# Tokens scaled ahead of their transposes, the first two products interleaved, and the residual's scale taken out later

## Chip, cores and metric

One core of one Trainium2 chip runs the kernel. The metric is the device time of one execution in microseconds (us). Before the change the median of three runs is 1152.77 us (1152.27 to 1153.73).

## What is computed

One inference step of a two-layer decoder for 512 prompt tokens and 8 x 8 sample tokens, 576 columns in all, with 1024 features. Layer A is a gated linear recurrence of 16 heads of 128 keys and 128 values; then come one shared key/value projection, layer B (sliding-window attention over it) and a last norm. What the change touches is the entry into layer A:

```python
def rms_norm(x, g):
    y = x * lax.rsqrt(jnp.mean(x * x, axis=-1, keepdims=True) + EPS)
    return y * g
def hgrn2_layer(x, s0, w_in, w_out, g_norm, g_onorm, lb):
    q, fz, i, gate = jnp.split(rms_norm(x, g_norm) @ w_in, 4, axis=-1)
    logf = jnp.logaddexp(jnp.log(lb), jnp.log1p(-lb) + jax.nn.log_sigmoid(fz))
    k = (1.0 - lb) * jax.nn.sigmoid(-fz)
    q = jax.nn.silu(q) * A_HEAD_K ** -0.5
    o, s_new = hgrn2_recurrence(heads(q), heads(k), heads(i), heads(logf), s0)
    o = rms_norm(o, g_onorm) * jax.nn.silu(gate)
    return x + o @ w_out, s_new
```

The last line needs the residual x itself, not the normed x.

## The kernel before

Activations lie with features on partitions: hT, xhi and xlo are 128 x 8 x 576 (8 feature tiles k, 576 columns in two halves j of 288). A product with a 1024 x 128 slice of weights is made of three terms of rounded numbers: whi·xhi, whi·xlo and wlo·xhi, 8 tiles by 2 halves each, 48 matmuls of 128 x 288. The weights come by SP's DMA queue into a tile raw (three buffers); ACT rounds it to whi (line 205) and DVE takes wlo = raw - whi (line 209). In layer B, wlo is made by another way: ACT writes -whi, and a DMA that POOL issues adds raw to it (lines 202 and 203).

The beginning (lines 154 to 306): SP loads three token blocks xt of 128 x 1024, six small vectors into vecs, two more token blocks, then weights. `arrive(i)` sums a block's squares on ACT, transposes the raw block on PE in eight pieces (px, line 281), copies them to hT on DVE (line 282), turns the sum into the reciprocal root q on ACT (lines 283 and 284), and spreads q along the columns of rall: a diagonal dg on DVE (line 286), multiplied with ones on PE (pr, line 288), copied by ACT (line 289). `normed(j)` then makes, for each k of a half, u = hT·norm_a·rall on DVE (line 296), xhi on ACT (line 297) and xlo = u - xhi on DVE, or on POOL for k in 1, 4, 7 (line 298):

```python
        for k in range(KT):
            u = stp.tile([P, HN], F32, tag="u", name=f"u{j}_{k}", bufs=4)
            dve.scalar_tensor_tensor(u, hT[:, k, r], vec("norm_a", k), rall[:, r], ALU.mult, ALU.mult)
            act.copy(xhi[:, k, r], u)
            (pool if k in LO_POOL else dve).tensor_tensor(xlo[:, k, r], u, xhi[:, k, r].bitcast(F32), ALU.subtract)
```

`head_main(h)` makes a head's four products, pf (forget), pq (query), pi (value) and pg (gate), each with its elementwise work: from pf come ka, lf, the sums Xl (five adds on POOL, line 611) and a scan NB; from pq comes KQ. Head 0's pf is made half by half, all other products with both halves in turn. `head_rec(h)` is the recurrence of a head: the factors G and KL, E, kd, Qz and KQ·E on DVE and ACT, then small matmuls (pa, poT, psO, pus). It is woven with head_main(h + 1), so that PE makes the next head's products between the small matmuls. The output of a head is normed per token: ACT squares psO and poT into `on` with a sum (line 900), takes Ln and Exp (lines 901 and 902), and scales psO and poT into `on` (line 904), which also ends their use of PSUM; the pool of PSUM tiles named psx has three buffers, which px, poT, psO, pus and others share. The second pus takes the buffer that psO held. A scheduler in the framework orders each engine's instructions by readiness and by priorities that the code gives; `tc.issue_after(x)` puts work behind the instruction x on the same engine. Every engine runs its list in order. After every fourth head the residual is brought up to date (hT += po, line 443).

## Time and profile before

| | |
|---|---|
| median of 3 runs | 1152.77 us |
| profiled execution: its own time | 1152.44 us |
| profiled execution: span of the profile | 1150.6 us |
| mean granted TensorE clock | 0.987 |
| PE, DVE, ACT, POOL busy | 1105.9, 857.6, 749.4, 265.9 us |

The span is the part of the profiled execution that the trace covers; its own time is 1.84 us longer. PE is the matmul engine, DVE, ACT and POOL do elementwise work, SP issues most DMAs. Rows of a timeline say when an instruction (or xN of a kind in a row) starts, how long it takes, the engine, the line of the code, what it writes and reads, and in brackets how long the engine had been idle before it and what ended that. "PEclk" is the granted share of the full TensorE clock.

### The profile page before, as it was taken

The numbers are of one execution on the slowest core, as the hardware profiler recorded it, in microseconds if no ns is written. First come the engines' busy times: TensorE is split into PE (matmuls) and PEld (weight loads), VectorE is DVE, ScalarE is ACT, GpSimd is POOL, SyncE is SP. The second block draws the span as 40 slices with busy tenths as digits, with TensorE's granted clock in tenths as the row PEclk, the third lists the DMA queues.
The fourth block names the chain that finished last, engine by engine and source line by source line (L and its number), as shares of the span: only waits on it lengthen the run. The fifth ranks groups of instructions, "written<-read, shape, count | busy, mean of one in ns | idle before, by whom it ended". The sixth has DMA issues, their size and how long they took to land.

```text
span 1150.6 us, 27472 instructions
## 1 busy us (share of the span) xinstructions
PE 1105.9 (96%) x10937; PEld 1072.6 (93%) x10937; DVE 857.6 (75%) x2090; ACT 749.4 (65%) x1748; POOL 265.9 (23%) x311
## 2 busy tenths in 40 slices
...
GB/s 157 93 113 78 104 94 113 77 79 108 71 118 107 122 87 110 89 76 107 96 71 110 86 77 92 143 137 117 132 114 126 129 128 134 126 127 113 127 111 83
DMA packets 168010, 123.19 MB, mean 107 GB/s; under 512 B 4665, under 2 KB 158314, under 8 KB 167850
## 3 DMA queue, kind: packets, MB, share of 16 engines
...
q14 instruction: 42, 0.34, 0.1%
...
## 4 chain that ended last, share of the span: by engine, by line
PE 51%; DVE 6%; ACT 3%; issue 1%; DMA 1%; POOL 0%; DVEq 0%; POOLq 0%; ACTq 0%
PE pbg L216 8%; PE pbq L216 8%; PE po L216 6%; PE po L233 4%; PE pg L233 3%; PE pf L233 3%; PE pi L233 3%; PE pq L233 2%; PE sc L1103 2%; PE pkv L216 2%; PE pav L1186 1%; PE pz L216 1%; PE pa L802 1%; PE ptr L1154 1%; DMA wlo_o<-raw_o 1%
## 5 line engine op out<-in xcount | busy, mean ns | idle before, releaser
L205 ACT CAST whi_a<-raw_a 128x1024 fp32r<-128x1024 f32 x64 | 67.1, 1049 | 66.8 <-PE po L233 32.3
L209 DVE TENSOR_TENSOR wlo_a<-raw_a,whi_a 128x1024 fp32r<-128x1024 f32 x64 | 81.8, 1284 | 24.6 <-issue 23.2
L611 POOL TENSOR_TENSOR Xl<-Xl 128x72 f32<-128x72 f32 x80 | 49.6, 649 | 207.0 <-DVE Xl L608 205.7
L643 POOL TENSOR_TENSOR sg<-sg,lg 128x576 f32<-128x576 f32 x16 | 26.2, 1638 | 279.3 <-ACT lg L576 279.3
L1132 ACT ACTIVATE P<-P,st 128x192 f32<-128x192 f32 (+2 forms) x128 | 54.1, 424 | 38.4 <-DVE st L1127 38.3
L1141 POOL TENSOR_SCALAR P<-P,st 128x192 f32<-128x192 f32 (+1 forms) x64 | 47.9, 754 | 93.6 <-DVE st L1134 76.8
L443 DVE TENSOR_TENSOR hT<-hT,po 128x576 f32<-128x576 f32 x32 | 24.1, 754 | 51.0 <-PE po L233 50.7
L233 PE MATMUL po<-oh,whi_o 128*128 128x288 f32 x256 | 42.8, 302 | 4.4 <-ACT whi_o L205 1.9
L216 PE MATMUL po<-ohb,wlo_o 128*128 128x288 f32 x224 | 41.1, 297 | 2.2 <-DMA wlo_o<-raw_o 2.1
L667 POOL TENSOR_TENSOR vb<-vst,bmask 128x512 fp32r<-128x512 f32 x32 | 36.7, 1166 | 26.7 <-DVE vst L663 13.8
L216 PE MATMUL po<-ohb,whi_o 128*128 128x288 f32 x224 | 42.0, 302 | 0.2
L216 PE MATMUL pbq<-xhi,wlo_bq 128*128 128x256 f32 (+1 forms) x256 | 39.9, 297 | 2.4 <-DMA wlo_bq<-raw_bq 2.4
L233 PEld LDWEIGHTS po<-oh,whi_o 128*128 128x128 f32 x256 | 35.9, 188 | 6.4 <-ACT whi_o L205 2.2
L216 PE MATMUL po<-olb,whi_o 128*128 128x288 f32 x224 | 41.4, 298 | 0.5 <-DVE olb L1400 0.4
L233 PE MATMUL po<-ol,whi_o 128*128 128x288 f32 x256 | 41.4, 299 | 0.0
L233 PE MATMUL po<-oh,wlo_o 128*128 128x288 f32 x256 | 41.1, 298 | 0.0
L216 PE MATMUL pbq<-xhi,whi_bq 128*128 128x256 f32 (+1 forms) x256 | 40.5, 300 | 0.0
L216 PE MATMUL pbg<-xhi,whi_bg 128*128 128x288 f32 x256 | 40.5, 300 | 0.0
L216 PE MATMUL pbq<-xlo,whi_bq 128*128 128x256 f32 (+1 forms) x256 | 39.3, 296 | 0.0
L233 PE MATMUL pf<-xhi,wlo_a 128*128 128x288 f32 x256 | 37.5, 299 | 1.8 <-DVE wlo_a L209 1.8
L216 PE MATMUL pbg<-xhi,wlo_bg 128*128 128x288 f32 x256 | 39.1, 295 | 0.0
L233 PE MATMUL pf<-xhi,whi_a 128*128 128x288 f32 x256 | 39.1, 303 | 0.0
(390 smaller groups left out, 3676.7 us busy)
## 6 DMA issues: line engine op xcount, KB each, us to landing
...
```

Source lines behind the costliest of these rows:

```text
L205: act.copy(hi[:, :n], raw[:, :n])
L209: eng.tensor_tensor(lo[:, r], raw[:, r], hi[:, r].bitcast(F32), ALU.subtract)
L216: pe.matmul(pm[:, : c1 - c0], w[:, k * width + w0 : k * width + w0 + P], x(k)[i][:, c0:c1], start=n == 0, stop=n == len(terms) - 1,)
L233: pe.matmul(pm[:, j, :HN], w[:, k * width + c0 : k * width + c0 + P], x(k, j), start=n == 0 and k == 0, stop=n == 2 and k == nk - 1,)
L443: dve.tensor_add(h2, h2, ps2(pm))
L611: pool.tensor_tensor(X8[:, :, j : j + 1], X8[:, :, j : j + 1], X8[:, :, k : k + 1], ALU.add)
L643: (pool if SGP else dve).tensor_tensor(sg, sg, l, ALU.mult)
L667: pool.tensor_tensor(t, view(vst.bitcast(F32), [[0, 4], [1, P]], off=half * P), view(bmask, [[1, 4], [0, P]]), ALU.mult,)
L802: pe.matmul(pa[32 * j : 32 * j + ns, c, t0 : t0 + nt], keys[:, c * P + s0 : c * P + s0 + ns], queries[:, c * P + t0 : c * P + t0 + nt], st ...
L1103: pe.matmul(sc[:, hf, k0[hf] :], QS[pr][:, 2 * n + hf, :], kk[:, g, ks], start=q == 0, stop=q == 1)
L1132: act.activation(x, x, AF.Exp, bias=st[:, a : a + 1], accum_out=st[:, 8 + a : 9 + a])
L1141: (pool if e == "p" else dve).tensor_scalar(x, x, st[:, 8 + a : 9 + a], None, ALU.mult)
```

## The change

The vector norm_a is loaded by itself behind the first token block, and the first two weight slices ahead of the other vectors. Each token block is multiplied by its q in place, tokens on partitions, before it is transposed, so that hT holds normed tokens. xhi is then one ACT instruction from hT with norm_a as scale, and xlo one DVE instruction. wlo of head 0's first two slices is made by ACT and a POOL DMA, as in layer B. Head 0's pf and pq are interleaved by k in the first half. The small constants on DVE are put behind the last xlo. rall now holds 1/q; it is made after pq, and hT gets its scale back in 16 multiplications of 128 x 288, four in each of heads 0 to 3.

```diff
--- before.py
+++ after.py
@@ -67,7 +67,6 @@
-LO_POOL = (1, 4, 7)
@@ -157,29 +156,36 @@
         sp.dma_start(xt[:n, :], tokens(i))
         xts.append(xt)
 
-    for i in range(3):
+    load_tokens(0)
+    vec_a = stp.tile([KT, P], F32, name="vec_a")
+    sp.dma_start(vec_a, norm_a.rearrange("o (k p) -> (o k) p", p=P))
+    for i in range(1, 5):
         load_tokens(i)
 
+    raws = {}
+    for part in (1, 0):
+        src = w_in_a[0, :, part * DI : part * DI + P].rearrange("(k p) c -> p k c", p=P)
+        raws[f"a0_{part}"] = wts.tile([P, 1024], F32, tag="raw", name=f"raw_a0_{part}", bufs=3)
+        sp.dma_start(raws[f"a0_{part}"].rearrange("p (a c) -> p a c", a=KT), src)
+
+
     vecs = stp.tile([64, P], F32, name="vecs")
-    dve.memset(vecs, 0.0)
-    row = 0
-    vcol = {}
+    pool.memset(vecs, 0.0)
+    row = KT
+    vcol = {"norm_a": (0, KT)}
     for name, ap, n in (
-        ("norm_a", norm_a.rearrange("o (k p) -> (o k) p", p=P), KT),
         ("norm_kv", norm_kv.rearrange("(k p) -> k p", p=P), KT),
         ("norm_b", norm_b.rearrange("o (k p) -> (o k) p", p=P), KT),
         ("norm_f", norm_f.rearrange("(k p) -> k p", p=P), KT),
         ("lb", lower_bounds_a.rearrange("o (k p) -> (o k) p", p=P), NH),
         ("onorm", onorm_a, 1),
     ):
-        sp.dma_start(vecs[row : row + n, :], ap)
+        sp.dma_start(vecs[row - KT : row - KT + n, :], ap)
         vcol[name] = (row, n)
         row += n
-    for i in range(3, 5):
-        load_tokens(i)
     snk = cst.tile([P, NHB], F32, name="snk")
     sp.dma_start(snk, bass.AP(tensor=sinks_b.tensor, offset=sinks_b.offset, ap=[[0, P], [1, NHB]]))
-    vT = cst.tile([P, 64], F32, name="vT")
+    vT = cst.tile([P, KT + 64], F32, name="vT")
 
     def vec(name, i):
         r, _ = vcol[name]
@@ -268,91 +274,120 @@
     rts = [rall[:, j * HN : (j + 1) * HN] for j in range(2)]
     ssq = cst.tile([P, 5], F32, name="ssq")
 
+    def to_tokens(i, after):
+
+        n = P if i < 4 else LS
+        q = ssq[:n, i : i + 1]
+        junk = stp.tile([P, D], F32, tag="junk", name=f"junk{i}", bufs=2)
+        act.activation(junk[:n], xts[i][:n], AF.Square, accum_out=q)
+        act.activation(q, q, AF.Ln, bias=eps_c[:n], scale=1.0 / D)
+        act.activation(q, q, AF.Exp, scale=-0.5)
+        with ExitStack() as when:
+            if after:
+                when.enter_context(tc.issue_after(after))
+            dve.tensor_scalar(xts[i][:n], xts[i][:n], q, None, ALU.mult)
+
     def arrive(i):
 
         n = P if i < 4 else LS
-        xt, q = xts[i][:n], ssq[:n, i : i + 1]
         r = slice(i * P, i * P + n)
-        junk = stp.tile([P, D], F32, tag="junk", name=f"junk{i}", bufs=2)
-        act.activation(junk[:n], xt, AF.Square, accum_out=q)
         for c in range(0, KT, 4):
             px = misc(f"px{i}_{c}").rearrange("p (k t) -> p k t", k=4)[:, :, :n]
             for k in range(4):
-                pe.transpose(px[:, k, :], xt[:, (c + k) * P : (c + k + 1) * P], ident[:n, :n])
-            dve.tensor_copy(hT[:, c : c + 4, r], px)
-        act.activation(q, q, AF.Ln, bias=eps_c[:n], scale=1.0 / D)
-        act.activation(q, q, AF.Exp, scale=-0.5)
-        dg = stp.tile([P, P], F32, tag="dg", name=f"dg{i}", bufs=2)
-        dve.tensor_scalar(dg[:n, :n], ident[:n, :n], q, None, ALU.mult)
-        pr = half(f"pr{i}")
-        pe.matmul(pr[:, :n], ones[:n, :], dg[:n, :n], start=True, stop=True)
-        act.copy(rall[:, r], pr[:, :n])
-
-    def normed(j):
+                pe.transpose(px[:, k, :], xts[i][:n, (c + k) * P : (c + k + 1) * P], ident[:n, :n])
+            last = dve.tensor_copy(hT[:, c : c + 4, r], px)
+        return last.ins
+
+    def normed(j, ks):
 
         r = slice(j * HN, (j + 1) * HN)
-        for k in range(KT):
-            u = stp.tile([P, HN], F32, tag="u", name=f"u{j}_{k}", bufs=4)
-            dve.scalar_tensor_tensor(u, hT[:, k, r], vec("norm_a", k), rall[:, r], ALU.mult, ALU.mult)
-            act.copy(xhi[:, k, r], u)
-            (pool if k in LO_POOL else dve).tensor_tensor(xlo[:, k, r], u, xhi[:, k, r].bitcast(F32), ALU.subtract)
-
-    for i in range(3):
+        for k in ks:
+            high = act.activation(xhi[:, k, r], hT[:, k, r], AF.Copy, scale=vec("norm_a", k))
+            low = dve.scalar_tensor_tensor(
+                xlo[:, k, r], hT[:, k, r], vec("norm_a", k), xhi[:, k, r].bitcast(F32), ALU.mult, ALU.subtract
+            )
+        return high.ins, low.ins
+
+    def high(name):
+
+        hi, lo = [wts.tile([P, 1024], F32R, tag=t, name=f"{t}_{name}") for t in ("whi", "wlo")]
+        act.copy(hi, raws[name])
+        return hi, lo
+
+    def low(name, hi, lo):
+        act.activation(lo, raws[name], AF.Copy, scale=-1.0)
+        pool.dma_start(lo.bitcast(F32), raws[name], accum_op=ALU.add)
+
+    pv = misc("pva")
+    pe.transpose(pv[:, :KT], vec_a, ident[:KT, :KT])
+    dve.tensor_copy(vT[:, :KT], pv[:, :KT])
+    came = []
+    for i in range(5):
+        to_tokens(i, came[i - 2] if i > 1 else None)
+        if i < 3:
+            came.append(arrive(i))
+    w0 = {1: high("a0_1")}
+    normed(0, range(3))
+    w0[0] = high("a0_0")
+    first, _ = normed(0, range(3, KT))
+    with tc.issue_after(first):
+        low("a0_1", *w0[1])
+    for i in range(3, 5):
         arrive(i)
+    low("a0_0", *w0[0])
+    _, second = normed(1, range(KT))
     pv = misc("pv")
     pe.transpose(pv[:, :64], vecs, ident[:64, :64])
-    dve.tensor_copy(vT, pv[:, :64])
-    normed(0)
-    for i in range(3, 5):
-        arrive(i)
-    normed(1)
-
...
     si = cst.tile([P, P], I32, name="si")
     ti = cst.tile([P, P], I32, name="ti")
     pool.iota(si, [[0, P]], base=0, channel_multiplier=1)
     pool.iota(ti, [[1, P]], base=0, channel_multiplier=0)
-
...
+    with tc.issue_after(second):
...
     amask = cst.tile([P, W], F32, name="amask")
@@ -580,14 +615,59 @@
             c = part * DI + h * P
             return split_weights(w_in_a[0, :, c : c + P].rearrange("(k p) c -> p k c", p=P), f"a{h}_{part}")
 
+        def again():
+
+            for i in range(5):
+                n = P if i < 4 else LS
+                if i in (0, 4):
+                    pr = misc(f"pr{i}")
+                c = i % 4 * P
+                pe.matmul(pr[:, c : c + n], ones[:n, :], dg[:n, i * P : i * P + n], start=True, stop=True)
+                if i > 2:
+                    act.copy(rall[:, i // 4 * LP : (i + 1) * P if i < 4 else T], pr[:, : c + n])
+
+        dg = tt("dg")
+        with tc.issue_after(second):
+            dve.reciprocal(ssq[:, :4], ssq[:, :4])
+            dve.reciprocal(ssq[:LS, 4:], ssq[:LS, 4:])
+            for i in range(5):
+                n = P if i < 4 else LS
+                dve.tensor_scalar(dg[:n, i * P : i * P + n], ident[:n, :n], ssq[:n, i : i + 1], None, ALU.mult)
+
+        def first_two():
+
+            pms = {p: main(f"p{'qf'[p]}0") for p in (1, 0)}
+
+            def terms(p, j, ws):
+                for k, w, x in ws:
+                    pe.matmul(
+                        pms[p][:, j, :HN],
+                        w0[p][w][:, k * P : (k + 1) * P],
+                        xview((xhi, xlo)[x])(k, j),
+                        start=k == 0 and w == 0 and x == 0,
+                        stop=k == KT - 1 and (w, x) == ((1, 0), (0, 1))[j],
+                    )
+
+            for k in range(KT):
+                for p in (1, 0):
+                    terms(p, 0, [(k, 0, 0), (k, 0, 1)])
+            for p in (1, 0):
+                terms(p, 0, [(k, 1, 0) for k in range(KT)])
+                terms(p, 1, [(k, w, x) for k in range(KT) for w, x in ((0, 0), (1, 0), (0, 1))])
+            return pms[1], pms[0]
+
         def head_main(h, st):
             KQ = wk.tile([P, 2, T], F32, tag="KQ", name=f"KQ{h}", bufs=2)
             NB = wk.tile([P, 2, T], F32, tag="NB", name=f"NB{h}", bufs=2)
             st["KQ"], st["NB"] = KQ, NB
 
-            w = weights_in(h, 1)
-            pf = main(f"pf{h}")
-            yield from product(pf, *w, xview(xhi), xview(xlo), order=((0, 1),) if h else ((0,), (1,)))
+            if h:
+                w = weights_in(h, 1)
+                pf = main(f"pf{h}")
+                yield from product(pf, *w, xview(xhi), xview(xlo))
+            else:
+                pf, pq = first_two()
+                again()
             with early():
                 l = tt(f"lf{h}")
                 act.activation(s2(l), ps2(pf), AF.Abs)
@@ -612,9 +692,10 @@
             dve.tensor_tensor_scan(NB[:, 1, :], rmask, lf, 0.0, ALU.mult, ALU.add)
             yield
 
-            w = weights_in(h, 0)
-            pq = main(f"pq{h}")
-            yield from product(pq, *w, xview(xhi), xview(xlo))
+            if h:
+                w = weights_in(h, 0)
+                pq = main(f"pq{h}")
+                yield from product(pq, *w, xview(xhi), xview(xlo))
             with early():
                 q = KQ[:, 1, :]
                 l = silu_arg(pq, q, f"q{h}")
@@ -818,7 +899,7 @@
                     stop=True,
                     tile_position=(0, 32 * j),
                 )
-            dve.copy_predicated(att, view(m_ge, [[0, NC], [1, P]]), pa)
+            st["mark"] = dve.copy_predicated(att, view(m_ge, [[0, NC], [1, P]]), pa).ins
             ats = att_s[i2]
             dve.copy_predicated(
                 view(ats[:LS, :], [[32, 4], [1, 16]]),
@@ -974,6 +1055,11 @@
             woven(head_rec(h, st, outs), itertools.chain(*chunks), n)
             for make in {5: (prompt_mask,), 6: (sample_mask,), 7: (sink_rows,)}.get(h, ()):
                 make()
+            if h < 4:
+                with tc.issue_after(st["mark"]):
+                    for j in range(4):
+                        x = hT[:, 2 * h + j // 2, j % 2 * HN : j % 2 * HN + HN]
+                        dve.tensor_tensor(x, x, rts[j % 2], ALU.mult)
             st = nxt
         out_scaled(w_out_a, NH - 4 + FILL, outs[FILL:], "norm_kv", tt)
         share[0] = LO_KV
```

The order of the instructions, at three places.

PE at the beginning (px: transposed token blocks; pr: q spread over columns; xt_88 is block 0, xt_92 and xt_94 are blocks 1 and 2, xt_96 and xt_98 blocks 3 and 4). Before, from the third block on:

```order
L281 MATMUL px_0_158<-ident,xt_92 128x128 x4
L281 MATMUL px_4_164<-ident,xt_92 128x128 x4
L288 MATMUL pr_174<-dg_172,ones 128x128
L303 MATMUL pv<-ident,vecs 128x64
L281 MATMUL px_0_214<-ident,xt_102 128x128 x4
L281 MATMUL px_4_220<-ident,xt_102 128x128 x4
L281 MATMUL px_0_235<-ident,xt_104 128x64 x4
L281 MATMUL px_4_241<-ident,xt_104 128x64 x4
L288 MATMUL pr_230<-dg_228,ones 128x128
L288 MATMUL pr_251<-dg_249,ones 128x64
L233 MATMUL pf_382<-xhi,whi_a_1_378 128x288 x8
```

After, from the third block on:

```order
L297 MATMUL px_0_161<-ident,xt_94 128x128 x4
L297 MATMUL px_4_167<-ident,xt_94 128x128 x4
L643 MATMUL pf_350<-xhi,whi_a_1_183 128x288
L297 MATMUL px_0_207<-ident,xt_96 128x128 x4
L297 MATMUL px_4_213<-ident,xt_96 128x128 x4
L297 MATMUL px_0_219<-ident,xt_98 128x64 x4
L643 MATMUL pf_350<-xlo,whi_a_1_183 128x288
L643 MATMUL pq_351<-xhi,whi_a_0_192 128x288
L643 MATMUL pq_351<-xlo,whi_a_0_192 128x288
L643 MATMUL pf_350<-xhi,whi_a_1_183 128x288
```

The first product starts behind three blocks instead of five, the pr matmuls are gone from here, and pf and pq take turns.

DVE from head 0's factor KL on, up to wlo of head 1's forget weights, on which the last third of pf of head 1 waits (wlo_a_1 in both). Before:

```order
L736 TENSOR_TENSOR G_0_668<-G_0_668,KQ_374 128x512
L736 TENSOR_TENSOR G_0_672<-G_0_672,KQ_374 128x512
L743 SCALAR_TENSOR_TENSOR KL_676<-KL_676,KQ_374 128x576
L748 TENSOR_TENSOR E_681<-NB_375,OFF_362 128x512 x2
L768 TENSOR_TENSOR kd_686<-KQ_374,E_681 128x256
L774 TENSOR_TENSOR Qz_356<-KQ_374,E_681 128x4x2x8
L209 TENSOR_TENSOR wlo_a_1_695<-raw_a_1_692,whi_a_1_694 128x1024
L568 TENSOR_SCALAR sg_626<-pg_577 128x576
L780 TENSOR_TENSOR KQ_374<-KQ_374,E_681 128x2x512
L663 TENSOR_TENSOR vst_643<-pvs_640,vst_643 32x256 x2
```

After:

```order
L829 TENSOR_TENSOR E_652<-NB_349,OFF_328 128x512
L817 TENSOR_TENSOR G_0_639<-G_0_639,KQ_348 128x512
L829 TENSOR_TENSOR E_652<-NB_349,OFF_328 128x512
L817 TENSOR_TENSOR G_0_643<-G_0_643,KQ_348 128x512
L603 TENSOR_SCALAR sg_597<-pg_548 128x576
L849 TENSOR_TENSOR kd_657<-KQ_348,E_652 128x256
L855 TENSOR_TENSOR Qz_322<-KQ_348,E_652 128x4x2x8
L861 TENSOR_TENSOR KQ_348<-KQ_348,E_652 128x2x512
L215 TENSOR_TENSOR wlo_a_1_666<-raw_a_1_663,whi_a_1_665 128x1024
L744 TENSOR_TENSOR vst_614<-pvs_611,vst_614 32x256 x2
```

wlo_a_1 stood ahead of sg and of the multiplication KQ·E; it now stands behind both.

ACT around the output norm `on` of head 0, while PE makes head 1. Before:

```order
L576 ACTIVATE lq_920<-lq_920 128x576
L900 ACTIVATE on_985,rs_986<-psO_972 128x128
L900 ACTIVATE on_985,rs_986<-poT_967 128x128 x4
L901 ACTIVATE rs_986<-rs_986,eps_c 128x5
L902 ACTIVATE rs_986<-rs_986 128x5
L904 ACTIVATE on_985<-psO_972,rs_986 128x128
L904 ACTIVATE on_985<-poT_967,rs_986 128x128 x4
L205 CAST whi_a_1_1186<-raw_a_1_1184 128x1024
```

After:

```order
L611 ACTIVATE lq_891<-lq_891 128x576
L806 ACTIVATE G_1_1126<-G_1_1126 128x4x2x32
L981 ACTIVATE on_956,rs_957<-psO_943 128x128
L981 ACTIVATE on_956,rs_957<-poT_938 128x128 x4
L816 ACTIVATE G_1_1135<-G_1_1135 128x512
L982 ACTIVATE rs_957<-rs_957,eps_c 128x5
L816 ACTIVATE G_1_1139<-G_1_1139 128x512
L983 ACTIVATE rs_957<-rs_957 128x5
L211 CAST whi_a_1_1161<-raw_a_1_1159 128x1024
L985 ACTIVATE on_956<-psO_943,rs_957 128x128
L985 ACTIVATE on_956<-poT_938,rs_957 128x128 x4
```

Between the squares and the scaling of psO now stand two exponentials of G and a rounding of weights; the same holds in the recurrences of heads 1 to 3, and from head 4 on the order is as before.

## Rows read from the trace of the kernel before

**Rows 1.** The page, part 1: busy time of each engine in us, its share of the span, and the number of its instructions.

```profile
PE 1105.9 (96%) x10937; PEld 1072.6 (93%) x10937; DVE 857.6 (75%) x2090; ACT 749.4 (65%) x1748; POOL 265.9 (23%) x311
```

**Rows 2.** Windows of 30 us, all engines: length, busy us of PE, PEld, DVE, ACT and POOL with the number of instructions, PEclk, DMA share, GB/s.

```profile
0.00:30.00 30.00, 17.12 (x83) 14.97 (x84) 25.56 (x71) 18.85 (x45) 5.75 (x14) 0.77 0.52 151
30.00:60.00 30.00, 30.00 (x300) 29.80 (x299) 25.64 (x52) 21.20 (x38) 6.14 (x8) 1.00 0.34 97
60.00:90.00 30.00, 30.00 (x317) 29.31 (x316) 27.24 (x52) 21.41 (x51) 7.47 (x8) 1.00 0.40 116
90.00:120.00 30.00, 30.00 (x390) 29.12 (x389) 25.57 (x50) 21.19 (x47) 5.39 (x8) 1.00 0.32 92
```

**Rows 3.** What PE waited for, over the whole span: total us, times, longest.

```profile
PE pr L288 <- DVE dg L286: 6.6, 1, 6.6
...
PE pf L233 <- DVE wlo_a L209: 1.8, 3, 1.4
```

**Rows 4.** Timeline of PE up to head 1.

```profile
4.44 1.94 PE L281 MATMUL px<-ident,xt 128*128 128x128 f32 x8 [4.44 <-DMA xt<-in_x_prompt_dram]
...
13.01 2.52 PE L281 MATMUL px<-ident,xt 128*128 128x128 f32 x16
22.13 1.48 PE L288 MATMUL pr<-dg,ones 128*128 128x128 f32 x4 [6.61 <-DVE dg L286]
23.54 2.29 PE L233 MATMUL pf<-xhi,whi_a 128*128 128x288 f32 x8
...
38.53 2.29 PE L233 MATMUL pi<-xhi,whi_a 128*128 128x288 f32 x16
40.66 2.30 PE L233 MATMUL pi<-xlo,whi_a 128*128 128x288 f32 x16
...
56.23 2.29 PE L233 MATMUL pf<-xhi,wlo_a 128*128 128x288 f32 x16
```

**Rows 5.** A window of PE at the beginning: length, PE busy, PEclk, DMA share, GB/s.

```profile
19.00:28.00 9.00, 5.81 (x22) 0.50 0.21 58
```

**Rows 6.** Timeline of ACT at the beginning and in head 0 (lines 283 and 284: Ln and Exp of a block's sum; 205: whi; 569: first of three for KQ; 740: first of two KL; 725: the inner G).

```profile
5.83 0.20 ACT L284 ACTIVATE ssq<-ssq 128x1 f32<-128x1 f32 x1
...
14.29 1.05 ACT L205 CAST whi_a<-raw_a 128x1024 fp32r<-128x1024 f32 x1 [0.79 <-DMA raw_a<-in_w_in_a_dram]
...
39.52 0.69 ACT L569 ACTIVATE lq<-KQ 128x576 f32<-128x576 f32 x1
...
45.02 0.69 ACT L740 ACTIVATE KL<-Xl 128x576 f32<-128x576 f32 x1 [3.38 <-POOL Xl L611]
...
46.18 1.03 ACT L205 CAST whi_a<-raw_a 128x1024 fp32r<-128x1024 f32 x1
...
48.75 0.44 ACT L725 ACTIVATE G<-G 128x256 f32<-128x256 f32 x1
```

**Rows 7.** Timeline of DVE: copies to hT, xlo, and head 0.

```profile
10.49 2.59 DVE L282 COPY hT<-px 128x512 f32<-128x512 f32 x4
...
25.25 0.45 DVE L298 TENSOR_TENSOR xlo<-u,xhi 128x288 fp32r<-128x288 f32 x1
...
38.73 0.76 DVE L568 TENSOR_SCALAR KQ<-pq 128x576 f32<-128x576 f32 x1 [1.58 <-PE pq L233]
39.54 0.82 DVE L604 SCALAR_TENSOR_TENSOR lf<-ka,ln1m,lf 128x576 f32<-128x576 f32 x1
...
41.41 0.30 DVE L608 TENSOR_SCALAR Xl<-lf 128x288 f32<-128x288 f32 x1
41.63 0.27 DVE L609 TENSOR_SCALAR Xl<-lf 128x216 f32<-128x216 f32 x1
...
50.25 1.29 DVE L736 TENSOR_TENSOR G<-G,KQ 128x512 f32<-128x512 f32 x2
51.45 0.75 DVE L743 SCALAR_TENSOR_TENSOR KL<-KL,KQ 128x576 f32<-128x576 f32 x1
...
53.32 0.42 DVE L768 TENSOR_TENSOR kd<-KQ,E 128x256 f32<-128x256 f32 x1
...
53.79 1.22 DVE L209 TENSOR_TENSOR wlo_a<-raw_a,whi_a 128x1024 fp32r<-128x1024 f32 x1
54.93 0.75 DVE L568 TENSOR_SCALAR sg<-pg 128x576 f32<-128x576 f32 x1
55.60 1.21 DVE L780 TENSOR_TENSOR KQ<-KQ,E 128x1024 f32<-128x1024 f32 x1
```

**Rows 8.** Timeline of POOL: the five adds to Xl of head 0.

```profile
41.79 3.19 POOL L611 TENSOR_TENSOR Xl<-Xl 128x72 f32<-128x72 f32 x5 [10.70 <-DVE Xl L608]
```

**Rows 9.** The tile wlo_bq of layer B, made by ACT and a POOL DMA: us from the DMA's issue to its landing, of sixteen such DMAs.

```profile
DMA to landing us min/median/max: 4.5/4.7/6.7
```

**Rows 10.** Timeline of PE in the recurrence of head 1: the last third of pf of head 2, which opens it, and the second pus.

```profile
90.01 2.29 PE L233 MATMUL pf<-xhi,wlo_a 128*128 128x288 f32 x16
...
111.65 0.40 PE L911 MATMUL pus<-vb,ks 128*128 128x512 f32 x1
```

**Rows 11.** Timeline of ACT in the same recurrence: an exponential of G, the scaling of psO in the output norm, and the next whi.

```profile
103.85 0.61 ACT L735 ACTIVATE G<-G 128x512 f32<-128x512 f32 x1
...
109.49 0.37 ACT L904 ACTIVATE on<-psO,rs 128x128 f32<-128x128 f32 x1
...
110.75 1.07 ACT L205 CAST whi_a<-raw_a 128x1024 fp32r<-128x1024 f32 x1
```

80 lines of the change are left out of this document (41 added, 39 removed).

## The prediction

> **What bounds the kernel now.** I read the busy times first: PE works 1105.9 us of a span of 1150.6 [rows 1], and in the windows of 30 us from the second on it works all 30.00 of each [rows 2]. So in the first heads whatever delays PE lengthens the kernel, and only the first window (17.12 us busy) has something to give. The waits of PE name it: 6.6 us in one piece, for DVE's dg [rows 3]. The timeline puts it in place: the transposes start at 4.44, the last 16 at 13.01, pr of the last blocks waits until 22.13, and the first product starts at 23.54 [rows 4]. Ahead of that DVE makes copies, u, xlo and dg in one list, so the products start late because DVE's list is long. [...] The profiled execution took 1152.44 us, 0.33 below the median of the runs; the sums below are against it.
>
> **The beginning, with the change.** Block 0's Exp ends at 5.83 + 0.20 = 6.03 on ACT [rows 6], and the next blocks follow before DVE gets to them. The new work is one scaling of 128x1024 on DVE per block. The trace has none of this size. The near shapes from SBUF take 0.30 for 288 columns and 0.27 for 216 [rows 7], 0.0004 to 0.0005 a column, which extends to 0.6 to 0.7 for 1024; the multiplication of 1024 columns with two tensors (1.21) is the other end. I take 0.7, since the near rows are of the same operation. DVE then does, in the order shown: two scalings, two copies (0.65 each, from 2.59 for four [rows 7]), a third scaling, four copies, two more scalings: from block 0's transposes, which end near 8.9 (6.9 plus 1.94 for eight [rows 4]), to 14.4. The weights' whi is ready by then: raw landed at 14.29 before [rows 6], and the two slices now stand ahead of five small loads. From 14.4 xlo follows xhi at the pace of 0.45 [rows 7] to 18.3, and each k feeds four matmuls. PE's first steady products start near 16.6, against 23.54.
>
> The next limit is wlo. ACT copies the first slice behind the eight xhi, to 17.9; then the POOL DMA takes 4.7 us (4.5 to 6.7) from issue to landing [rows 9]: 22.6. The 32 matmuls of the first half end by then, if PE is at its full clock: 16 matmuls take 2.13 there (38.53 to 40.66 [rows 4]), 0.133 each. The other 64 matmuls of the two products take 8.5, to 31.2; the second half's xlo is there by 24.8 (four copies, then eight at 0.45). Five pr matmuls add about 0.9 (half of the low-clock 1.48 for four, scaled to five [rows 4]). pi starts at 32.2, not 38.53: **6.3 us earlier**.
>
> [...]
>
> **Where half of it goes again.** pf of head 1 needs wlo of its weights, and DVE's list has this behind KQ·E and sg now, not ahead. PE would ask for it 56.23 - 38.53 = 17.7 after pi's start [rows 4], at 49.9. DVE's chain: pq ends at 31.2, KQ takes 0.76 [rows 7]; ACT rounds the gate's weights (1.05) and makes three steps for KQ at 0.7 [rows 6], two copies of rall and two steps for ka of that size, to about 36.9; lf (0.82) and Xl (0.5 [rows 7]) end at 38.2, the five adds on POOL take 3.19 [rows 8], to 41.4; two KL, three copies and the G's on ACT take 3.1 (45.02 to 49.19 before, less a whi of 1.03 [rows 6]), to 44.5. From there DVE does six multiplications or subtractions at 0.60, two more of G (0.60), sg 0.67, kd and Qz 0.47, KQ·E 1.24 and wlo 1.2 (all from starts to next starts [rows 7]): 8.4, to 52.9. **PE waits 3.0 us**; pf's last third starts at 52.9 where it was at 56.23, so 3.3 us of gain are left. In the trace before, such waits come to 1.8 us in three places, the longest 1.4 [rows 3].
>
> **Heads 0 to 3.** Sixteen multiplications bring hT back: 128x288 with two tensors, 0.45 each [rows 7], 1.8 us of DVE per head. DVE has room (25.57 busy of 30.00, 27.24 in one window [rows 2]), but the order moves: on ACT two exponentials of G (0.61 each) and a whi (1.07) stand between the squares and the scaling of psO [rows 11]. That scaling ended at 109.49 + 0.37 = 109.86, 19.85 after pf's last third started at 90.01; with 2.29 more it ends 22.1 after. The second pus takes psO's buffer, and PE asks for it at 111.65, 21.64 after [rows 10]. PE loses 0.5 (0 if the exponentials come early, 1.2 if DVE feeds them late) in each of four heads: **2.1 us**. From head 4 on the orders agree, and I cost the rest at nothing: the small constants lie on DVE while PE does the 64 matmuls, and ACT's two steps for wlo take the place of two on DVE. Without that cover each would cost its 1.2 us.
>
> **Sum.** 6.3 - 3.0 - 2.1 = 1.2 us: 1152.44 - 1.2 = 1151.2; against the median it would be 1151.6. I keep 1151.2.
>
> **Rivals.**
> - *The gain is kept.* If the exponentials of G end before the squares do, pus never waits: 3.3 us, 1149.1. For it: psO's scaling had 1.8 us to spare before [rows 10, 11], and ACT has 9 us free in 30 [rows 2]. Against: ACT runs its list in order, and whi stands ahead in any case.
> - *wlo of head 1 comes earlier than I walk it,* by shorter waits between POOL, ACT and DVE: up to 6.3 - 2.1 = 4.2 us, 1148.2. Against: the chain has been costed from durations alone, with few gaps.
> - *The clock stays low longer.* The first 32 matmuls are now paced by xlo, with pauses, where before eight followed eight at a time. If they run at 0.26 each (half speed, as from 19 to 28 us [rows 5]) they end at 25.0 and not by 22.6: 2.4 us later, 1153.6. For it: PEclk was 0.50 while PE was busy 5.81 of 9.00 us [rows 5]. [...]
> - *DVE becomes the bound in heads 0 to 3: slower.* The four multiplications stand ahead of the subtractions that feed G. If their 1.8 us pass through whole, psO's scaling comes 2.3 late in each head, 9.2 in all, against 3.3 gained: up to 5.9 slower, 1158.3. It decides from 0.8 us per head on (0.2% from 1.4). For it: 27.24 of 30 busy in one window [rows 2]. Against: 25.57 in the next, and the wait for lq on ACT that covers part of it.
>
> **How the numbers follow.** About 0.2% (2.3 us) can be told from no change. My forecast, with its own range of 1150.4 to 1153.0, has a chance of 0.37; the low clock 0.10, inside the 0.2% as well: 0.47 for the same. The kept gain, which takes only one early exponential per head, has 0.26, and the early wlo, which takes a chain of several engines, 0.15: 0.41 for faster. DVE as the bound has 0.12, which is slower. The range leaves out the slow case and the sum of both faster rivals (6.3 us, 1146.1): from 1147.0, 1.2 us beyond the better of them alone, to 1154.2, the low clock with 0.6 more of waits.
>
> **What would show it.** Right: the first product near 16.6 us, pi near 32, no wait on dg, a wait of about 3 us of PE on wlo_a near 50, and four waits of about 0.5 on ACT's `on` in front of pus. Wrong: wlo landing after 25, a PEclk of 0.50 beyond 22 us, no wait on `on`, or PE below 29.5 busy of 30 in the windows from 60 to 180.

## The result, and the profile after

The changed kernel is a little slower, not faster. Beside the kernel before on the same chips, 14 runs of each, it takes 1156.3 us in the median (1152.76 to 1159.14) against 1153.76 (1150.66 to 1155.82): a ratio of **1.0022, interval 1.0013 to 1.0031**. The forecast was 1151.2, and 1154.2 at most. The profiled execution took 1155.74, with a span of 1154.0 where before had 1150.6. Single executions of either kernel differ by several us, so places are compared by traces and totals by ratios.

The page, part 1, as in [rows 1]:

```profile
PE 1106.3 (96%) x10938; PEld 1071.3 (93%) x10938; DVE 856.8 (74%) x2101; ACT 751.8 (65%) x1747; POOL 268.9 (23%) x308
```

PE is busy 0.4 us longer than before, so 3.0 of the 3.4 us of longer span are waits. The windows of 30 us, with the columns of [rows 2], say which stretch has them:

```profile
0.00:30.00 30.00, 19.42 (x97) 17.09 (x98) 22.94 (x75) 20.71 (x44) 3.21 (x12) 0.94 0.74 186
30.00:60.00 30.00, 28.38 (x285) 27.75 (x284) 24.22 (x42) 21.07 (x37) 7.00 (x8) 1.00 0.35 97
60.00:90.00 30.00, 28.29 (x304) 27.51 (x304) 26.57 (x55) 20.33 (x50) 5.85 (x6) 1.00 0.38 108
90.00:120.00 30.00, 29.56 (x383) 28.46 (x382) 24.97 (x51) 20.19 (x47) 7.81 (x8) 1.00 0.29 84
```

The first window gained 2.3 us of PE's work, and each of the next three lost some: 1.6, 1.7 and 0.4. DVE has no window at 27. What PE waited for, in us, times and longest, to hold against [rows 3]:

```profile
PE pf L239 <- DVE wlo_a L215: 3.5, 4, 1.6
...
PE smg L894 <- issue: 1.7, 1, 1.7
PE pf L643 <- ACT xhi L305: 1.6, 1, 1.6
PE pus L992 <- issue: 1.5, 4, 0.5
...
PE pf L643 <- DMA wlo_a<-raw_a: 1.3, 1, 1.3
```

The wait on dg, 6.6 in one piece, is gone. Five kinds of smaller waits stand in its place (only the first was there before, with 1.8), two of them called "issue", where the releaser is not in the profile. The timeline of PE puts them in place (start, length, idle time before it; it answers to [rows 4] and [rows 10]):

```profile
15.40 0.61 PE L643 MATMUL pf<-xhi,whi_a 128*128 128x288 f32 x1 [1.60 <-ACT xhi L305]
15.80 2.52 PE L297 MATMUL px<-ident,xt 128*128 128x128 f32 x12
18.26 0.61 PE L643 MATMUL pf<-xlo,whi_a 128*128 128x288 f32 x1
...
23.67 0.40 PE L643 MATMUL pq<-xlo,whi_a 128*128 128x288 f32 x1
25.35 1.66 PE L643 MATMUL pf<-xhi,wlo_a 128*128 128x288 f32 x8 [1.28 <-DMA wlo_a<-raw_a]
...
35.49 1.42 PE L625 MATMUL pr<-dg,ones 128*128 128x128 f32 x10
36.83 2.39 PE L239 MATMUL pi<-xhi,whi_a 128*128 128x288 f32 x16
...
56.42 2.38 PE L239 MATMUL pf<-xhi,wlo_a 128*128 128x288 f32 x16 [1.62 <-DVE wlo_a L215]
...
64.76 0.31 PE L894 MATMUL smg<-KL 128*32 128x64 f32 x4 [1.71 <-issue]
...
114.28 0.47 PE L992 MATMUL pus<-vb,ks 128*128 128x512 f32 x1 [0.44 <-issue]
```

Read down against before: pi of head 0 starts 1.70 earlier (36.83, it was 38.53), pf's last third of head 1 0.19 **later** (56.42, it was 56.23), and pi of head 1 2.14 later (70.80, it was 68.66), behind the stop of 1.71 at smg. Then three heads with a wait at pus lose 0.64 to 0.68 each (34.35 us from pi of head 2 to pi of head 3, it was 33.68); at head 5 the lag is 4.02 (235.74 against 231.72). At the end it is 3.4. Some of this last step is chance: both kernels wait 1.93 us for whi_o near 382 and 386, and before's clock fell there (0.83 from 380 to 390), the change's did not (1.00).

The beginning in ACT's timeline, where [rows 6] had block 0's Exp and the first whi:

```profile
7.29 1.06 ACT L282 ACTIVATE junk<-xt 128x1024 f32<-128x1024 f32 x1 [1.07 <-DMA xt<-in_x_prompt_dram]
...
13.88 1.03 ACT L314 CAST whi_a<-raw_a 128x1024 fp32r<-128x1024 f32 x1
14.82 1.38 ACT L305 ACTIVATE xhi<-hT,vT 128x288 fp32r<-128x288 f32 x3
16.11 1.03 ACT L314 CAST whi_a<-raw_a 128x1024 fp32r<-128x1024 f32 x1
17.04 2.24 ACT L305 ACTIVATE xhi<-hT,vT 128x288 fp32r<-128x288 f32 x5
19.19 1.99 ACT L318 ACTIVATE wlo_a<-raw_a 128x1024 fp32r<-128x1024 f32 x2
```

ACT has no gap from 13.88 on; two whi and eight xhi stand ahead of wlo, whose first copy ends near 20.2. POOL's timeline has the DMA behind it:

```profile
20.54 1.94 POOL L319 DMA_DIRECT2D wlo_a<-raw_a  x2 [18.68 <-ACT wlo_a L318]
```

From its issue at 20.54 to PE's start at 25.35 are 4.8 us, inside [rows 9]. Then the clock (length, PE busy, PEclk, DMA share, GB/s, as [rows 5]):

```profile
24.00:26.00 2.00, 0.72 (x6) 1.00 1.04 197
26.00:30.00 4.00, 4.00 (x21) 0.57 0.95 206
```

In the 4 us behind the wait PE made 21 matmuls; from 26.5 to 29.5 us the granted clock was 0.50. DVE's timeline, for [rows 7]: the scaling of a block, and what stands ahead of wlo of head 1.

```profile
6.25 0.75 DVE L288 TENSOR_SCALAR xt<-xt,ssq 128x1024 f32<-128x1024 f32 x1 [1.39 <-ACT ssq L284]
...
54.01 1.21 DVE L861 TENSOR_TENSOR KQ<-KQ,E 128x1024 f32<-128x1024 f32 x1
55.15 1.22 DVE L215 TENSOR_TENSOR wlo_a<-raw_a,whi_a 128x1024 fp32r<-128x1024 f32 x1
```

And ACT in the recurrence of head 1, for [rows 11]: the second exponential of G and a whi ahead of the scaling of psO.

```profile
112.27 0.62 ACT L816 ACTIVATE G<-G 128x512 f32<-128x512 f32 x1
...
112.88 1.04 ACT L211 CAST whi_a<-raw_a 128x1024 fp32r<-128x1024 f32 x1
113.83 0.35 ACT L985 ACTIVATE on<-psO,rs 128x128 f32<-128x128 f32 x1
```

That scaling ends at 114.18, and pus starts at 114.28. So the wait that the profile calls "issue" is the one on psO's buffer.

Of the prediction's signs of being wrong, three came: wlo's landing after 25 us, a PEclk of about 0.50 beyond 22 us, and PE below 29.5 busy of 30 in a window from 60 us on. Of its signs of being right, the wait on dg is gone and pus waits about 0.5, three times instead of four.

### The profile page after: what moved, and what is told of

It reads as the page before. It is cut to its first block, busy times and chain, and to the rows that moved or that the text cites. A ratio compares the mean times of both kernels' runs of the same rounds, so it can differ in the third digit from the quotient of the medians.

```text
span 1154.0 us, 27477 instructions
## 1 busy us (share of the span) xinstructions
PE 1106.3 (96%) x10938; PEld 1071.3 (93%) x10938; DVE 856.8 (74%) x2101; ACT 751.8 (65%) x1747; POOL 268.9 (23%) x308
## 3 DMA queue, kind: packets, MB, share of 16 engines
q8 instruction: 86, 1.41, 0.5%
## 4 chain that ended last, share of the span: by engine, by line
PE 45%; DVE 8%; ACT 6%; issue 2%; DMA 1%; POOL 1%; DVEq 0%; POOLq 0%; ACTq 0%
PE pbg L222 7%; PE po L222 6%; PE pbq L222 5%; PE po L239 4%; PE pg L239 3%; PE pf L239 3%; PE pi L239 3%; PE pq L239 2%; PE pkv L222 2%; PE sc L1189 2%; ACT P L1218 2%; PE pav L1272 1%; PE pz L222 1%; PE pa L883 1%; DVE P L1193 1%
## 5 line engine op out<-in xcount | busy, mean ns | idle before, releaser
L215 DVE TENSOR_TENSOR wlo_a<-raw_a,whi_a 128x1024 fp32r<-128x1024 f32 x62 | 79.0, 1278 | 28.7 <-issue 25.3
L724 POOL TENSOR_TENSOR sg<-sg,lg 128x576 f32<-128x576 f32 x16 | 25.3, 1580 | 208.9 <-ACT lg L611 208.9
L748 POOL TENSOR_TENSOR vb<-vst,bmask 128x512 fp32r<-128x512 f32 x32 | 41.5, 1319 | 94.4 <-DVE vst L744 94.4
L222 PE MATMUL pbg<-xlo,whi_bg 128*128 128x288 f32 x256 | 39.1, 294 | 0.0
L1193 DVE CUSTOM_DVE_ANT_0 P<-sc,amask 128x192 f32<-128x192 f32 (+2 forms) x128 | 36.4, 328 | 3.3 <-PE sc L1189 2.9
```

What stands on the lines that cost most here:

```text
L215: eng.tensor_tensor(lo[:, r], raw[:, r], hi[:, r].bitcast(F32), ALU.subtract)
L222: pe.matmul(pm[:, : c1 - c0], w[:, k * width + w0 : k * width + w0 + P], x(k)[i][:, c0:c1], start=n == 0, stop=n == len(terms) - 1,)
L724: (pool if SGP else dve).tensor_tensor(sg, sg, l, ALU.mult)
L748: pool.tensor_tensor(t, view(vst.bitcast(F32), [[0, 4], [1, P]], off=half * P), view(bmask, [[1, 4], [0, P]]), ALU.mult,)
L1193: dve.tensor_tensor_reduce(Pt[:, pr, hf, k0[hf] :], sc[:, hf, k0[hf] :], amask[:, k0[hf] :], 0.125, NEG, ALU.add, ALU.max, accum_out=st[:, ...
```

## The experiments

Each was timed in five rounds beside the kernel before; "pi" is the start of pi of head 0.

What the beginning does by chance has to be known first. In eight traces it is the changed kernel's own (the profile after, e1, e2, e4, e5, e7, e9, e12), and yet the first product starts anywhere from 15.29 to 16.81 us, as the token blocks land earlier or later (ACT gets block 1 at 7.29 us in the profile after and at 8.03 in e7), and pi from 35.25 to 37.97. From the first product to pi it takes 19.9 us in four of them and 21.4 in the other four, in which the clock fell behind the landing of wlo. Those two numbers, not pi alone, are what an edit to the beginning has to be held against.

### e1: the changed kernel once more

> The changed kernel once more, to tell what of its trace repeats. In its first profile PE stopped for 1.7 us in front of smg at 64.8 us, with no semaphore that it waited for, and before head 0's first wlo terms the DMA was waited for 1.3 us, after which PEclk fell to 0.50 for three us. Theory A (the order of the instructions costs the time): the waits on wlo_a near 56 us (1.6) and in front of pus in three heads (0.45 each, 0.67 with what hangs on them) come again to 0.1 us, the stop before smg too if it is bound to the place in the program. Rival B (chance): the stop before smg or the fall of the clock is gone, and the start of pi of head 1 (70.8) is up to 2 us earlier. Time: 1.000 to 1.004 of before.

1155.48 us against 1152.24, ratio 1.0032 (1.0020 to 1.0044). The waits are the same: 1.53 for wlo's landing, 1.62 on wlo_a of head 1, 1.36 at smg, three of 0.46 to 0.48 at pus; pi 36.70. The loss is real and stands in the same places.

### e2: the 16 multiplications left out

The residual isn't scaled back, so what layer A's output adds to is the normed hT.

```diff
-            if h < 4:
-                with tc.issue_after(st["mark"]):
-                    for j in range(4):
-                        x = hT[:, 2 * h + j // 2, j % 2 * HN : j % 2 * HN + HN]
-                        dve.tensor_tensor(x, x, rts[j % 2], ALU.mult)
```

> Leaves out the 16 multiplications that give hT its scale back (the residual is then wrong). ACT's order in heads 0 to 3 is then squares, Ln, Exp, scaling of psO, whi, as in the kernel before. Theory A (the place of these multiplications moves ACT's order, and that costs): no wait in front of pus, pi to pi 33.7 us in every head as before, 2.0 us less than the changed kernel, ratio to before about 1.0005. Rival B (pus waits because the heads now lie later against DVE's and ACT's work, from the beginning on): the waits of 0.45 stay, ratio 1.002.

1152.7 us against 1152.24, ratio 1.0004 (0.9990 to 1.0017). No wait at pus is left, and a head lasts 33.67 us (pi of heads 2 and 3 at 103.71 and 137.38). The loss in heads 1 to 3 hangs on the multiplications alone. pf's wait on wlo_a of head 1 stays. It is 2.25 there, and behind it the clock fell (0.57 from 55.4 to 59.2 us): the 16 matmuls took 3.81 us instead of 2.38.

### e3: the same 16 multiplications in the kernel before

```diff
+    one_h = cst.tile([P, HN], F32, name="one_h")
+    pool.memset(one_h, 1.0)
...
-            dve.copy_predicated(att, view(m_ge, [[0, NC], [1, P]]), pa)
+            st["mark"] = dve.copy_predicated(att, view(m_ge, [[0, NC], [1, P]]), pa).ins
...
+            if h < 4:
+                with tc.issue_after(st["mark"]):
+                    for j in range(4):
+                        x = hT[:, 2 * h + j // 2, j % 2 * HN : j % 2 * HN + HN]
+                        dve.tensor_tensor(x, x, one_h, ALU.mult)
```

> The kernel before, with 16 multiplications of hT by a tile of ones at the same places (four in each of heads 0 to 3, behind the copy of att); the beginning is untouched. Theory A: ACT's order becomes that of the changed kernel in these heads (on's scaling behind two exponentials of G and a whi), and pus waits about 0.45 us in three or four heads: 2.0 to 2.7 us more than before, 1.0020. Rival B (only the changed beginning makes pus late): no wait, 1.0000, since DVE has 3 to 4 us free in 30.

1154.46 us against 1152.24, ratio 1.0018 (1.0008 to 1.0028). Its beginning is before's (pi 38.47), and yet it waits at pus, 0.99 in the first recurrence and 0.45 in the next. Its timelines of PE and ACT have the changed kernel's order:

```profile
113.63 0.47 PE L913 MATMUL pus<-vb,ks 128*128 128x512 f32 x1 [0.45 <-issue]
```

```profile
112.23 1.04 ACT L207 CAST whi_a<-raw_a 128x1024 fp32r<-128x1024 f32 x1
113.18 0.35 ACT L906 ACTIVATE on<-psO,rs 128x128 f32<-128x128 f32 x1
```

So work on DVE that nobody waits for costs 2.2 us in the medians (3.4 by pi of head 5 in the trace), by the order that it makes on ACT.

### e4: head 1's forget weights at a higher priority

```diff
+W1 = 100
...
-                w = weights_in(h, 1)
+                with early(W1 if h == 1 else 0):
+                    w = weights_in(h, 1)
```

> The changed kernel with head 1's forget weights split at a higher priority: wlo_a of head 1 then stands on DVE behind the first subtraction of NB, ahead of KL, G, sg and KQ times E, instead of behind all of them. Theory A (wlo_a's place behind the chain took what the beginning gained): the wait of 1.6 us in front of pf's last third is gone and all after it is 1.6 us earlier, ratio 0.9986 of the changed kernel. Rival B (the chain is late itself): G, KL and E come 1.2 us later, and PE waits for them in front of pa instead: no change.

1157.04 us (5 runs) against 1152.24, ratio 1.0045 (1.0033 to 1.0057): worse. The wait on wlo_a is gone and pi of head 1 comes at 68.77, but DVE's later work meets POOL's. DVE's timeline, and POOL's below it:

```profile
56.66 1.06 DVE L857 TENSOR_TENSOR Qz<-KQ,E 128x64 f32<-128x64 f32 x1
57.64 2.08 DVE L216 TENSOR_TENSOR wlo_a<-raw_a,whi_a 128x1024 fp32r<-128x1024 f32 x1
59.64 2.43 DVE L863 TENSOR_TENSOR KQ<-KQ,E 128x1024 f32<-128x1024 f32 x1
```

```profile
56.42 2.22 POOL L750 TENSOR_TENSOR vb<-vst,bmask 128x512 fp32r<-128x512 f32 x2 [10.30 <-DVE vst L746]
58.60 2.39 POOL L726 TENSOR_TENSOR sg<-sg,lg 128x576 f32<-128x576 f32 x1
```

The same operations took 0.21, 1.22 and 1.21 in the changed kernel, and POOL's sg, 2.39 here, has a median of 1.43 over its sixteen. ka comes at 63.24 instead of 60.96, and PE waits 1.34 for kt and 0.96 at pus of the first recurrence: the gain turned into other waits.

### e5: the multiplications behind ol

They are kept whole, and only put later in DVE's list.

```diff
-            st["mark"] = dve.copy_predicated(att, view(m_ge, [[0, NC], [1, P]]), pa).ins
+            dve.copy_predicated(att, view(m_ge, [[0, NC], [1, P]]), pa)
...
-            dve.tensor_tensor(ol, osb, oh.bitcast(F32), ALU.subtract)
+            st["mark"] = dve.tensor_tensor(ol, osb, oh.bitcast(F32), ALU.subtract).ins
```

> The changed kernel with the four multiplications of each of heads 0 to 3 behind the subtraction ol at the recurrence's end, not behind the copy of att. ACT's list is then that of the kernel before there (squares, Ln, Exp, scaling of psO, whi). Theory A (ACT's order in front of pus costs 0.67 us in three heads): no wait in front of pus, 2.0 us less than the changed kernel, ratio to before about 1.001. Rival B (what the leaving out gave back in the run before was the work itself): 1.003 as the changed kernel, with the 7 us of DVE now late for wlo and kd of the next head.

1154.11 us against 1152.33, ratio 1.0006 (0.9991 to 1.0020). There are no waits at pus, and a head lasts 33.69 (a stop at smg is left, 0.70). In ACT's timeline the scaling now stands ahead of whi, and pus finds its buffer free:

```profile
108.98 0.37 ACT L985 ACTIVATE on<-psO,rs 128x128 f32<-128x128 f32 x1
...
110.24 1.08 ACT L211 CAST whi_a<-raw_a 128x1024 fp32r<-128x1024 f32 x1
```

```profile
111.14 0.40 PE L992 MATMUL pus<-vb,ks 128*128 128x512 f32 x1
```

DVE's time for them was never the cost; their place was. The profile tells two things more. PE's wait on wlo_a of head 1 is as long as in the profile after, though the beginning ended 1.6 us earlier (pq at 33.92, not 35.49):

```profile
54.84 2.38 PE L239 MATMUL pf<-xhi,wlo_a 128*128 128x288 f32 x16 [1.61 <-DVE wlo_a L215]
```

The other is the clock. Up to 25.3 us this beginning is e1's (first product 15.38, landing 25.32 behind a wait of 1.50), but the clock did not fall:

```profile
26.00:30.00 4.00, 4.00 (x32) 1.00 0.95 209
```

32 matmuls in those 4 us, not 21. From the landing the 64 matmuls took 8.60 us where e1 took 10.13, and pi came at 35.27 instead of 36.70: the fall of the clock behind the wait costs 1.5 us, and comes in some executions only.

### e6: wlo of head 0 by DVE

```diff
-        act.activation(lo, raws[name], AF.Copy, scale=-1.0)
-        pool.dma_start(lo.bitcast(F32), raws[name], accum_op=ALU.add)
+        dve.tensor_tensor(lo, raws[name], hi.bitcast(F32), ALU.subtract)
...
-    first, _ = normed(0, range(3, KT))
+    _, first = normed(0, range(3, KT))
```

> The changed kernel with wlo of head 0's first two slices made by DVE (raw minus whi, 1.2 us each, behind the first half's xlo and behind the copies of the last block) instead of by ACT and a POOL DMA. Theory A (the landing of that DMA holds up PE, and the pause lets the clock fall): no wait of 1.3 to 1.5 us near 24, no PEclk of 0.50 from 26 to 29, pi of head 0 near 34.5 and not 36.7; of these 2 us less than half is left at head 1's pf, since wlo_a there is late by its own chain. Rival B (DVE's two subtractions push the second half's xlo as far back as the DMA did): pi near 36.7 again.

1154.33 us against 1152.33, ratio 1.0011 (0.9995 to 1.0027): no difference from the changed kernel can be told. The wait for wlo fell to 0.26 and the clock stayed at 1.00, yet pi came at 37.78. Part of that is a late first product (16.96; ACT got block 1 only at 8.30), which the edit did not make. From there to pi it took 20.8, 0.9 more than the undisturbed 19.9, of which PE's wait for DVE's KQ is 0.78: the edit takes the wait away and gains nothing, as rival B had it in kind.

### e7: wlo of head 1 ahead of KQ·E, nothing else

```diff
-                w = weights_in(h, 1)
+                w = ahead["w"] if h == 1 else weights_in(h, 1)
...
-                dve.tensor_mul(KQ[:, :, :LP], KQ[:, :, :LP], E[:, :, :LP])
+                with ExitStack() as when:
+                    if h == 0:
+                        with tc.issue_after(z.ins):
+                            ahead["w"] = weights_in(1, 1)
+                        when.enter_context(tc.issue_after(ahead["lo"]))
+                    dve.tensor_mul(KQ[:, :, :LP], KQ[:, :, :LP], E[:, :, :LP])
```

(z is the multiplication that makes Qz, and ahead["lo"] the subtraction of wlo.)

> The changed kernel with one exchange in DVE's list: wlo_a of head 1's forget weights ahead of KQ times E of head 0, not behind it; sg and everything else stay. Theory A (its place costs): the wait of 1.62 in front of pf's last third falls to 0.5, and what follows is 1.1 us earlier, as long as KQ times E still ends before POOL's vb begins. Rival B (as when wlo stood far ahead: the chain of DVE, ACT and POOL behind it is the bound): the gain is taken back in front of smg, pu or pus, no change at pi of head 2.

1153.57 us against 1152.33, ratio 1.0016 (1.0002 to 1.0030). The wait of 1.62 fell to 0.55, there was no stop at smg, and pi of head 1 came at 67.73, 31.0 after pi of head 0 (34.0 in the changed kernel). The first recurrence took 1.5 of it back, 0.99 of that at pus (pi of head 2 at 102.95, 35.2 later), and the others lost as before. The repair works, but in this trace its gain passes on only if pus is repaired too.

### e8: norm_a's vector behind block 2

```diff
-    load_tokens(0)
+    for i in range(3):
+        load_tokens(i)
...
-    for i in range(1, 5):
+    for i in range(3, 5):
```

> The changed kernel with the load of norm_a behind the third token block and not behind the first. In the changed kernel block 1 was ready for ACT at 7.29 us, 5.94 before; one tiny load stands between, and four more big loads follow at once. Theory A (the small load's place delays block 1): block 1's squares start near 6, the first product and pi of head 0 1.0 to 1.3 us earlier. Rival B (the blocks share the DMA engines with the loads behind them): block 1 at 7.3 as before, pi near 36.7; or norm_a itself is late for the first xhi.

1154.3 us against 1152.33, ratio 1.0014 (1.0002 to 1.0027). Block 1 did come earlier, as theory A had it: its squares start at 5.86, not 7.29. But ACT then waited 0.49 and 0.95 for blocks 2 and 3, its first whi began at 13.94 (13.88 in the profile after), and wlo landed at 25.41 as before. PE had its first half done sooner, so its wait for the landing was 2.96; behind it the clock was 0.50 from 26 to 30, and pi came at 37.92. That block 1 waits behind a small load was not what held the start; the blocks behind it were.

### e9: e5 and e7 together

The edits are those of e5 and e7.

> The changed kernel with both repairs: hT's multiplications behind ol in heads 0 to 3, and wlo_a of head 1 ahead of KQ times E. Theory A (the two losses are separate and lie in the orders): no wait in front of pus, a wait of about 0.5 in front of pf's last third of head 1, pi of head 1 near 67.5 and of head 4 near 168.6, where the kernel before has 68.66 and 169.82: 1.2 us less than before, ratio 0.999. Rival B (what one repair gains the other wait takes): pi of head 4 at 169.8 or later, ratio 1.000 or more.

**1150.54 us against 1152.16, ratio 0.9983 (0.9972 to 0.9994): faster than before.** Nothing waits at pus or at smg, and pf's wait in head 1 is short:

```profile
54.28 2.38 PE L240 MATMUL pf<-xhi,wlo_a 128*128 128x288 f32 x16 [0.48 <-DVE wlo_a L216]
```

One new wait is there, 0.37 on DVE's S in the first recurrence, and the stretch from pi of head 1 to pi of head 2 takes 34.38 (33.78 before). pi of head 4 comes at 168.48, 1.3 ahead of before's 169.82 and 4.7 ahead of the changed kernel's 173.16.

### e10: e9, with wlo of head 0 copied directly behind its whi

```diff
     w0 = {1: high("a0_1")}
+    low("a0_1", *w0[1])
     normed(0, range(3))
...
-    with tc.issue_after(first):
-        low("a0_1", *w0[1])
```

> The same, with ACT's first step for wlo of head 0's forget weights directly behind whi, ahead of the xhi, so that its DMA starts 3 to 4 us earlier. Theory A (PE waits for the landing at 25.3 and the clock falls in that pause): no wait on wlo, no PEclk of 0.50 from 26 to 29, pi of head 0 near 34.5. Rival B (the second half's xlo, which ends at 27.2 on DVE, is the next bound): pi near 35.5, where it is without the fall of the clock.

1149.99 us against 1152.16, ratio 0.9981 (0.9968 to 0.9994), the same as e9. The wait for wlo is gone, yet pi came at 36.53 where e9 had 35.84. The copy now stands ahead of the xhi, which start 1.90 behind whi (0.93 in e9) and hold the first product back. From the first product to pi it took 19.8, the 19.9 of e9: taking the wait away gained nothing behind it. PE spends what it would have waited at the lower clock, which e9 has for a part of the same stretch:

```profile
16.70 0.61 PE L643 MATMUL pf<-xhi,whi_a 128*128 128x288 f32 x1 [3.40 <-ACT xhi L306]
```

```profile
20.00:23.00 3.00, 3.00 (x15) 0.50 0.32 66
```

(In e9 this window had 21 matmuls at 0.83.)

### e11: e10, with the first products ahead of the transposes of blocks 3 and 4

```diff
-    for i in range(3, 5):
-        arrive(i)
...
+    for k in range(KT):
+        for p in (1, 0):
+            m = terms(p, 0, [(k, 0, 0), (k, 0, 1)])
+        if k == 5:
+            held = m.ins
+    with tc.issue_after(held):
+        for i in range(3, 5):
+            arrive(i)
```

> The same as the one with the early step for wlo, and head 0's first products (up to the sixth feature tile of the first half) ahead of the transposes of blocks 3 and 4 on PE, not behind them. In the changed kernel these transposes hold PE from 15.8 to 18.3 while xlo is already there. Theory A (they hold up the products): the first half's 32 matmuls end near 21, pi near 33. Rival B (then block 3 and 4 are late for the second half, whose xlo is the bound): pi near 35 as without this step, or later.

1153.03 us against 1152.16, ratio 1.0010 (0.9999 to 1.0021): the repairs' gain is gone. pi came at 38.73: the first product was 1.2 later than in e10 by chance of the blocks (17.89; ACT got block 1 at 8.24, in e10 at 6.86), and from there it took 20.8, 1.0 more than in e10, since the copies of blocks 3 and 4 now wait for PE until 25.86 and the last xlo ends at 31.6. A stop of 1.84 at smg is back too. Taking the 12 transposes out of the first products does not make the start earlier.

### e12: the two raw loads beside smg taken apart

A memset of 128x8 holds back the load of head 2's forget weights.

```diff
+        if name == "a2_1":
+            with tc.issue_after(seam["smg"]), early(800):
+                dve.memset(raw[:, :8], 0.0)
```

(seam["smg"] is DVE's copy of head 0's smg.)

> The changed kernel, with one load moved: the raw slice of head 2's forget weights (the second of three loads of 512 KB that follow each other from 56.4 to 61.1 us on SP in the changed kernel) is made to wait for a small memset on DVE behind the copy of smg, so that it starts near 65.3 instead of right behind the load ahead of it. The order of all other instructions is that of the changed kernel. Theory A: PE's stop of 1.71 us ahead of smg (1.36 in the second profile of the same kernel) is its own instruction load, one packet of 16 KB of queue q8, which comes through late when it meets the seam of two raw loads. With no second load there, the stop is gone (0.2 us or less), and pi of head 1 starts 33.9 - 1.7 = 32.2 to 32.6 us after pi of head 0 (33.97 in the changed kernel, 33.62 in its second profile); the time falls by 1.4 to 1.7 us, to a ratio near 1.001 to 1.002. Theory B: the instruction load is late because PE asks for it late, whatever else moves; then the stop stays at 1.3 us or more and the time at a ratio of 1.002 to 1.003. Both expect no wait for head 2's weights, which have 20 us to spare; a wait of PE on wlo_a near 90 us would show that this is wrong.

1155.74 us against 1152.8, ratio 1.0020 (1.0007 to 1.0033): too wide to tell 1.5 us. The trace tells the step. Head 2's two first loads changed places on SP, so another load followed the first, but at 62.8 and not at once. First the changed kernel, 62 to 63 us, GB/s in slices of 25 ns and the queue of instructions; then this one, 61 to 62 us:

```profile
GB/s 103 102 143 82 123 123 184 82 164 82 123 102 143 82 778 82 82 82 102 123 41 82 61 61 164 164 164 143 143 143 123 123 102 102 123 123 123 164 123 164
...
q8 instruction: 1, 0.02, 5.9%
```

```profile
GB/s 41 20 20 0 0 0 655 0 0 0 0 0 0 0 0 0 0 0 0 0 0 0 0 0 0 0 0 0 0 0 0 0 0 0 0 0 0 0 0 0
...
q8 instruction: 1, 0.02, 6.0%
```

The peak is the packet of 16 KB of instructions: amid the traffic of two loads in the one (62.36; PE goes on at 64.76), alone in a gap in the other (61.15). And there PE does not stop:

```profile
64.00 0.24 PE L899 MATMUL smg<-KL 128*32 128x64 f32 x1
...
64.05 0.28 PE L899 MATMUL smg<-KL 128*32 128x64 f32 x3
...
70.07 2.22 PE L244 MATMUL pi<-xhi,whi_a 128*128 128x288 f32 x15
```

pi of head 1 starts 32.1 us after pi of head 0 (37.97), as theory A had it, where e1 had 33.6 and the profile after 34.0. pus of the first recurrence took 0.63 of it.

e12 is one profile, but the other traces bear it out. pf's wait on wlo_a of head 1 is not the cause: e12 has it (1.61) without a stop, e11 has the stop without it. In five traces (before, e4, e7, e9, e12) the packet starts 3.6 to 3.7 us behind the start of pf's last third of head 1; the loads moved 0 to 30 GB/s from 3.5 to 4.0 us behind that start, and PE doesn't stop. In four others (the profile after, e1, e2, e5) they moved 104 to 132 GB/s in that half us; the packet starts 4.9 to 6.1 us behind, smg starts 2.4 to 2.5 us behind the packet, and PE stops for 0.43 to 1.71.

## Why the prediction was wrong

**What bounds the kernel** was read rightly: PE's delays pass through to the end (a lag of 4.02 us at head 5, 3.4 at the end), and dg's wait could be taken away.

**The scaling of a block** (0.7 forecast) took 0.75; the time **from wlo's DMA to its landing** (4.7) took 4.8.

**The step that failed** is the sentence "ACT copies the first slice behind the eight xhi, to 17.9". From 14.4, eight xhi at 0.45 alone come to 18.0. The second whi (1.03), which stands amid them, and the copy itself (1.0) were not counted, and xhi began at 14.82. The copy ended near 20.2 and the landing came at 25.35, 2.75 after the forecast. ACT bounded this stretch, not DVE, whose list the prediction walked (and that list, redone from 8.9 with the prediction's own terms, ends at 14.9, not at 14.4). In nine traces with this order on ACT (the profile after, e1, e2, e4, e5, e7, e8, e9, e12) wlo's terms start 9.93 to 9.96 us behind the first product, wherever that lies. The early products did not matter: PE had used up the first half by 24.07 and waited 1.28.

Nor would a landing on time have given the 6.3 us: e6 and e10 have no such wait, and from the first product to pi they took 20.8 and 19.8, no less than the 19.9 with it. What bounds it then was not tested; next in line by its date is the second half's xlo, which was forecast to end at 24.8 and ended at 27.29, since DVE waited 1.61 for the last four transposes, which PE did amid the products.

**The clock.** 64 matmuls were forecast at 8.5 us and took 10.1, from 25.35 to 35.49. They take 8.6 where the clock stays up (e5), so its fall behind the landing costs 1.5. The rival of the low clock had it ahead of the landing. There the profile after ran at 1.00, but e1, e2, e4 and e5 at 0.50 to 0.55 from 17 to 20 us, and it cost them nothing, since the landing set the date. Five pr, forecast at 0.9, took 1.34: the 1.48 of [rows 4] are two pr, which the profile lists as two instructions each, and not four. So pi came at 36.83, not at 32.2 (2.75 for the landing, 1.5 for the clock, 0.3 for pr), and the gain there was 1.7, not 6.3. Without the fall of the clock it was 3.3 (e2 and e5, pi at 35.25 and 35.27).

**The wait on wlo_a of head 1** was right in kind, and the length of its chain too: from the end of pq to pf's last third 21.7 us were forecast, and it took 20.9 (35.49 to 56.42). Its parts agree as well: POOL's adds ended 9.8 behind pq (forecast 10.2), ACT's first G 12.5 (13.3), and DVE took 8.3 from there (8.4). Its root is another: not pq but the end of pf, 4.25 earlier, behind which ACT makes a whi and lf. From that whi (31.48) to pf's last third it takes 24.92 to 24.96 in six traces (the profile after, e1, e2, e5, e8, e12). So the chain sets a date that hangs on the beginning alone. pf and pq ended 4.3 late, and so 3.3 of forecast gain became 0.2 of loss. The wait itself doesn't depend on when the beginning ends: 1.61 to 1.64 in five of the six, with pq ending from 33.92 to 36.62. It was 1.62 instead of 3.0 because the chain was 0.8 shorter than forecast and PE asked for wlo_a 19.3 behind pq's end, not 18.7. In the sixth, e2, it was 2.25: there the small constants, costed at nothing, held that whi back by 0.6. e7 shows that the exchange on DVE makes this wait.

**Heads 0 to 3** went as forecast in kind, and the total is near: 2.1 us were set against four heads, and 0.64 to 0.68 were lost in three. That the totals agree is in part luck: each wait cost more than the 0.5 forecast, and the first recurrence had none because PE came there late, behind the stop at smg. Where that stop is missing and the order on ACT is the same, pus waits 0.37 to 0.99 there too (e3, e4, e6, e7, e12). The scaling of psO ended 22.1 us after pf's last third (114.18 and 92.06), the very number of the walk. e2, e3 and e5 show the cause from three sides. That DVE becomes the bound there is refuted by e5, which keeps the multiplications and loses nothing.

**The stop at smg**, 1.71 us (1.36 in e1), was not foreseen. No row of before hinted at it, since its packet of instructions had fallen between two loads, at 59.9, too. e12 shows the stop gone when the loads come apart, and the nine traces agree.

**The sum** at head 5: 0.2 lost at pf's last third, 1.9 to pi of head 1, of which the stop is 1.7, and 2.0 at pus make the 4.0 that the trace has there (0.1 was gained in head 1). Against the forecast of 1.2 gained, 3.5 of the 5.2 are the beginning and 1.9 the stretch with the stop, less 0.1 each in head 1 and at pus. Of what the medians lost (2.5 us), taking the waits at pus away gives most back: e2 and e5 are at 1.0004 and 1.0006. The exchange of wlo_a gives the rest and more (e9).

**What stays open:** why the clock fell behind the landing in the profile after, e1, e4 and e12, and not in e5 and e9, with waits of 1.28 to 1.57 in all six; why the token blocks land earlier or later (ACT gets block 1 from 6.86 to 8.30 us with the same order of loads); and how much of the stop at smg the medians hold.
